# Two modulation blocks as dots instead of matmuls, five more groups of seven products, more adding transfers and a table of buffer places

## The chip, the cores and the metric

The kernel runs on one core of a Trainium2 chip, in one launch. The metric is the time on the device in microseconds, the median of several runs. A profile of one execution is there too, with the start and duration of every instruction; its span goes from the first to the last instruction.

## What is computed

One inference step of a transformer layer for two groups of 128 tokens, a prompt (context) and a sample (latent), both of width 2048 and with the same weights, all in float32:

```python
def ada_mod(cvec, w_ada, b_ada):
    m = jax.nn.silu(cvec) @ w_ada + b_ada
    return jnp.split(m, 6, axis=-1)
...
        sh1, sc1, g1, sh2, sc2, g2 = ada_mod(c_ctx[None, None, :], w_ada[l], b_ada[l])
        h = rms_norm(xp, norm1_w[l]) * (1 + sc1) + sh1
        qa, ka, va, qb, kb, vb, ga, gb = project_heads(h, w_in[l], q_norm_a[l], k_norm_a[l],
                                                        q_norm_b[l], k_norm_b[l])
...
        oa = context_attention(qa, ka, va, sink)
        ob = context_attention(qb[:, :, :, None, :], kb, vb, None)
        xp = xp + g1 * merge_branches(oa, ob, ga, gb, w_br_a[l], w_br_b[l], w_out[l])
        h2 = rms_norm(xp, norm2_w[l]) * (1 + sc2) + sh2
        xp = xp + g2 * sq_relu_mlp(h2, w_up[l], w_down[l])
```

The sample goes the same way, with a rotary on mixer A, a windowed and a neighbourhood mask, and cached context keys. The weights are `w_ada` (2048 x 12288), `w_in` (2048 x 8704), two branches (1024 x 2048 each), `w_out` (2048 x 2048), `w_up` (2048 x 8192) and `w_down` (8192 x 2048). Their elements pass through the core once, apart from the adding transfers below, which read a tile a second time.

## The kernel before

**Steps.** The work on the large weights is a list of steps (`wsteps`). A plain step takes one tile of 128 x 1024 floats (512 KB): two blocks of 128 rows by 512 columns. float32 is made of two parts: ScalarE copies the tile `raw` to a rounded `wH` (L115), VectorE takes the difference `wL` = `raw` - `wH` (L275), and the activations are split alike. Each product is then three matmuls, high x high, low x high and high x low (L477 to L479, L350 to L352, L1453 to L1455). For two blocks and two token groups a plain step has twelve matmuls of 128 x 512. Steps 0 to 72 are the first nine units of `w_in`, then come the gates (to 135), the branches `ya` and `yb` (136 to 167), `w_out` (168 to 199), and pieces of `w_up` and `w_down` in turn.

**Groups of seven.** From the second piece on, and in the last piece of `w_down`, two column blocks are made together (`pair`). Eight times two row blocks stand there; for each, the products of 2 x 2 blocks are either made plainly (eight products, two plain steps) or with seven products of sums of blocks (Strassen's and Winograd's scheme; the steps `x` and `y`), where `FAST` names the position. The sums cost VectorE and ScalarE work: `XL`, `t`, two sums in `raw`, the halves of `YB`, and the splits of `t` and `u` (L1521 to L1543).

**Adding transfers.** Instead of the subtraction on VectorE, ScalarE can write -`wH` into the tile and a DMA from GpSimd's (POOL's) queue adds the weight from memory (`minus_plus`):

```python
        act.activation(lo, hi.bitcast(F32), AF.Copy, scale=-1.0)
        pool.dma_start(lo, src.bitcast(F32R), accum_op=OP.add)
```

`LO_DMA` names plain steps and how many steps ahead this begins, `XL_DMA` and `T_DMA` the positions and leads for `XL` and for a sum, `YL_DMA` positions for half of `YB`. An entry whose step is no group of seven, or is prepared already, does nothing.

**Modulation.** Scale and shift of both norms and the gates come from `w_ada`. Two ways are used. With matmuls (`pair_mm`, L368): for one block of 128 features 16 matmuls of 256 columns, four of them side by side in quarters of the array, into `ps_ada`, later evacuated, transposed (`ps_sel`, L386) and added up (`ada_cols`). With dots (`dot`, L1746): VectorE multiplies a transposed tile of 128 x 1024 with the broadcast condition and adds up, once for each half of the 2048 inputs and each token group. `FB_DVE` is the block of the second modulation from which dots take over, 6 of 16. `SS_G` and `SS_AT` place the matmul blocks before it, `DOTS` the dots, both by steps. Most are in the time of the gates, the branches and `w_out`; `dot_end` closes the scale.

**Order.** The order on each engine is the order in which the code records: at each step `run` issues the loads up to `RUN` steps ahead on SP's queue, prepares tiles up to `LOOK` steps ahead (and `wH` alone for `AHEAD` more), then the matmuls, then what is placed at that step (`at`, `ex`): the work of the attention (`POST`, `JOBS`), dots and transposes. At the end of `w_out` norm2 takes its sum of squares (L1274), POOL the root `r` (L1276), VectorE and ScalarE `h2f` (L1284), PE transposes it (`ps_h`, L1292), and the scale of the second modulation is applied.

**Buffers.** 54 buffers of 128 x 1024 floats form one ring (`gp`, tag "g"); each new tile takes the place that is next in turn and waits until the tile before it there is done.

Of the kernel before, what the change touches and what calls it, by code (L numbers as in the profile page):

```python
# [34 lines left out]
FB_DVE = 6  # L35
# [12 lines left out]
YL_DMA = [8, 9, 15, 23, 29, 31, 39, 67]  # L48
T_DMA = {15: 10, 48: 10, 55: 7, 64: 7, 65: 7, 66: 7, 67: 11}
# [28 lines left out]
DOTS2 = [225, 231, 234, 235, 237, 238, 245, 245, 258, 266, 268, 270, 270, 294, 300, 301, 306, 327, 328, 331, 333, 336, 349, 359, 360, 362, 363, 367, 394, 395, 396, 401]  # L78
STAT_AT = [2, -1, 9, 1]
T_PAIR = [[14, 4], [6, 9], [8, 8], [5, 8], [8, 9], [5, 10], [6, 14]]  # L80
P_PAIR = [[5, -1], [1, 1], [0, 5], [1, 5], [1, 6], [0, 5], [2, 2]]
M_TE = (3,)
M_AT = [1, 2, 6]
FLIP = 1
SOW_AT = 3
# [1837 lines left out]
```

## Time and profile before

| | |
|---|---|
| Median of 3 runs | 1312.15 us (1312.04 to 1312.45) |
| Span of the profiled execution, first to last instruction | 1310.0 us; its own time with what lies around the span is not listed apart from the runs |
| Granted TensorE clock | 0.999 |
| Moved by DMA | 401.16 MB, mean 306 GB/s |
| DMA from SP's queue (q1) | 387.36 MB, 81.5% of the time of 16 DMA engines |
| DMA from POOL's queue (q0) | 12.59 MB, 34 transfers, 28 of them adding |

A busy share is the part of the span in which an engine had an instruction under way. Matmuls overlap, so their start times tell their price rather than their durations. In a row of a group, the numbers behind the count are the busy time in us and the mean ns of one; behind the second bar stands the idle time just before, and what ended it. In a row of waits: who waited for whom, us in total, how often, the longest.

### The profile page before, as it was taken

What the parts mean: (1) busy time and instruction counts of PE and PEld (TensorE: products, weight loads), DVE (VectorE), ACT (ScalarE), POOL (GpSimd) and SP (SyncE); (2) the same over time, 40 slices, a digit from 0 to 9 for tenths busy, and PEclk for the clock granted to TensorE, in tenths of its full rate; (3) what the DMA queues carried; (4) which work ended last, traced back from release to release, by engine and by line L of the source; (5) the groups of instructions that cost most, each with busy time, mean ns of one, the idle gap of its engine ahead of it and who ended that gap; (6) DMA issues with size and microseconds to landing.
All of it is one profiled execution on the core that took longest, in us unless ns stands there. A gap on an engine that the chain in (4) does not pass through costs nothing.

```text
span 1310.0 us, 17956 instructions
## 1 busy us (share of the span) xinstructions
PE 1301.6 (99%) x6328; PEld 1057.2 (81%) x6328; DVE 1141.7 (87%) x1466; ACT 908.8 (69%) x1151; POOL 59.2 (5%) x68
## 2 busy tenths in 40 slices
PE   8999999999999999999999999999999999999998
PEld 4778788788888878888888888888888888888887
DVE  4669799989999999999779998987999988789776
ACT  5635566699866655636787778869779597697882
POOL 0000000332000000000000000000000000000010
PEclk9999999999999999999999999999999999999999
DMA  9999999997799979997599788778977978879972
GB/s 371 408 409 408 400 409 399 354 318 227 265 345 367 370 284 366 358 334 244 193 307 318 210 286 268 283 261 273 321 229 245 357 255 281 295 225 349 337 246 72
DMA packets 169995, 401.16 MB, mean 306 GB/s; under 512 B 71697, under 2 KB 72689, under 8 KB 169905
## 3 DMA queue, kind: packets, MB, share of 16 engines
q1 hardware_dynamic: 165312, 387.36, 81.5%
q0 software_dynamic: 4448, 12.59, 5.4%
q8 instruction: 49, 0.80, 0.2%
q14 instruction: 42, 0.34, 0.1%
q10 hardware_dynamic: 144, 0.08, 0.1%
HBM read 374.23 MB, written 10.80 MB: 294 GB/s over the span
## 4 chain that ended last, share of the span: by engine, by line
PE 97%; DMA 1%; ACT 1%; SPq 0%; DVE 0%; issue 0%; ACTq 0%
PE acc L350 16%; PE acc L351 16%; PE acc L352 16%; PE Q L1453 7%; PE Q L1455 7%; PE Q L1454 7%; PE acc L477 5%; PE acc L478 5%; PE acc L479 5%; PE ps_ada L368 3%; DMA araw<-in_w_pair 1%; PE Z L1455 1%; PE Z L1453 1%; PE Z L1454 1%; PE ps_S L922 1%; PE acc L1233 1%
## 5 line engine op out<-in xcount | busy, mean ns | idle before, releaser
L275 DVE TENSOR_TENSOR wL<-raw,wH 128x1024 fp32r<-128x1024 f32 x375 | 440.7, 1221 | 44.5 <-ACT wH L115 43.0
L115 ACT ACTIVATE wH<-raw 128x1024 fp32r<-128x1024 f32 (+1 forms) x390 | 384.6, 1038 | 60.4 <-DMA raw<-in_w_in 15.0
L477 PE MATMUL acc<-wH,hH 128*128 128x512 f32 x272 | 107.2, 394 | 0.6 <-ACT srow L115 0.6
L478 PE MATMUL acc<-wL,hH 128*128 128x512 f32 x272 | 106.0, 390 | 0.0
L479 PE MATMUL acc<-wH,hL 128*128 128x512 f32 x272 | 106.0, 390 | 0.0
L350 PE MATMUL acc<-wH,hH 128*128 128x512 f32 x252 | 101.3, 402 | 0.0
L351 PE MATMUL acc<-wL,hH 128*128 128x512 f32 x252 | 98.4, 390 | 0.0
L352 PE MATMUL acc<-wH,hL 128*128 128x512 f32 x252 | 98.3, 390 | 0.0
L115 ACT ACTIVATE uH<-raw 128x1024 fp32r<-128x1024 f32 x36 | 38.2, 1062 | 53.8 <-DVE raw L1540 33.5
L1746 DVE CUSTOM_DVE_ANT_0 aT<-aT,cB,cols 128x1024 f32<-128x1024 f32 x56 | 71.5, 1285 | 0.6
L1746 DVE CUSTOM_DVE_ANT_0 junk<-aT,cB,cols 128x1024 bf16<-128x1024 f32 x56 | 71.3, 1281 | 0.0
L477 PEld LDWEIGHTS acc<-wH,hH 128*128 128x128 f32 x272 | 51.1, 188 | 14.1 <-issue 2.9
L479 PEld LDWEIGHTS acc<-wH,hL 128*128 128x128 f32 x272 | 51.1, 188 | 10.8
L478 PEld LDWEIGHTS acc<-wL,hH 128*128 128x128 f32 x272 | 51.1, 188 | 10.2
L350 PEld LDWEIGHTS acc<-wH,hH 128*128 128x128 f32 x252 | 47.4, 188 | 10.6 <-issue 1.4
L351 PEld LDWEIGHTS acc<-wL,hH 128*128 128x128 f32 x252 | 47.4, 188 | 10.5 <-DVE wL L275 0.6
L352 PEld LDWEIGHTS acc<-wH,hL 128*128 128x128 f32 x252 | 47.3, 188 | 10.0
L115 ACT ACTIVATE tH<-t 128x1024 fp32r<-128x1024 f32 x31 | 32.8, 1057 | 27.3 <-DVE t L1532 23.6
L1746 DVE CUSTOM_DVE_ANT_0 aT<-aT,cB,gc_g 128x1024 f32<-128x1024 f32 x32 | 40.8, 1284 | 0.4
L1746 DVE CUSTOM_DVE_ANT_0 junk<-aT,cB,gc_g 128x1024 bf16<-128x1024 f32 x32 | 40.7, 1282 | 0.0
L115 ACT ACTIVATE fTa<-pTa 128x2048 uint16<-128x2048 uint16 x16 | 40.6, 2536 | 0.1
L1433 ACT ACTIVATE up<-up 128x1024 f32<-128x1024 f32 x28 | 29.7, 1062 | 15.4 <-DVE up L1580 14.9
(739 smaller groups left out, 3377.6 us busy)
## 6 DMA issues: line engine op xcount, KB each, us to landing
raw<-in_w_in SPq DMA_DIRECT2D x131, 512.0 KB, 8.7
raw<-in_w_down SPq DMA_DIRECT2D x124, 512.0 KB, 7.2
araw<-in_w_pair SPq DMA_DIRECT2D x80, 512.0 KB, 9.8
raw<-in_w_upF SPq DMA_DIRECT2D x68, 512.0 KB, 6.2
aT<-in_w_gT SPq DMA_DIRECT2D x64, 512.0 KB, 7.8
raw<-in_w_up SPq DMA_DIRECT2D x60, 512.0 KB, 6.7
aT<-in_w_adaT SPq DMA_DIRECT2D x48, 512.0 KB, 8.0
raw<-in_w_out SPq DMA_DIRECT2D x32, 512.0 KB, 8.7
```

What stands on the lines that cost most here:

```text
L115: act.activation(out, in_, AF.Copy)
L275: dve.tensor_tensor(st["lo"], st["raw"], st["hi"].bitcast(F32), op=OP.subtract)
L350: pe.matmul(acc[tb], sh, wh[:, k, :], start=f, stop=False, **kw)
L351: pe.matmul(acc[tb], sh, wl[:, k, :], start=False, stop=False, **kw)
L352: pe.matmul(acc[tb], sl, wh[:, k, :], start=False, stop=l, **kw)
L477: pe.matmul(acc[tb], sh, wh[:, k, :], start=kt == 0 and k == 0 and not held and not seeded, stop=False, **kw)
L478: pe.matmul(acc[tb], sh, wl[:, k, :], start=False, stop=False, **kw)
L479: pe.matmul(acc[tb], sl, wh[:, k, :], start=False, stop=last and k == 1 and not hold, **kw)
L1453: pe.matmul(acc, stat[0], hi, start=f, stop=False, **kw)
L1454: pe.matmul(acc, stat[0], lo, start=False, stop=False, **kw)
L1455: pe.matmul(acc, stat[1], hi, start=False, stop=l, **kw)
L1746: dve.tensor_tensor_reduce(out, box["raw"], cB[s, tag], 1.0, dst if second else baT[:, part, fb:fb + 1], OP.mult, OP.add, dst)
```

## The change

- `FB_DVE` 6 to 4: blocks 4 and 5 of the second modulation, 32 matmuls of `ps_ada` and four transposes, become 16 dots. The last dot stands at step 190, before it was 183. The four other blocks, two at step 53 and two at step 73, are now at steps 52, 53, 69 and 73.
- `FAST`: 39 groups of seven among the 56 of pieces 1 to 7, before 34.
- The tables of adding transfers name 33 more places; the built program issues 24 more (10 `wL`, 4 `XL`, 8 halves of `YB`, 2 sums), 52 adding transfers in place of 28.
- `HOMES`: each tile of the ring gets a place of its own from a table, instead of the next in turn.
- Side work: in three units the squares for QK-norm are added up by ScalarE as it squares, head by head, instead of a reduction on VectorE (`SSQ_ACT`); two of the eight softmax normalisations go from VectorE to ScalarE (`NORM_ACT`); `LOOK`, `RUN`, `AHEAD`, `POST`, `JOBS`, `DOTS`, `DOTS2` and some smaller tables have new numbers.

```diff
-FB_DVE = 6
+FB_DVE = 4
...
-YL_DMA = [8, 9, 15, 23, 29, 31, 39, 67]
-T_DMA = {15: 10, 48: 10, 55: 7, 64: 7, 65: 7, 66: 7, 67: 11}
+YL_DMA = [8, 9, 11, 15, 16, 20, 23, 24, 27, 30, 37, 39, 44, 54, 55, 56, 61, 64]
+T_DMA = {11: 11, 15: 10, 21: 10, 31: 8, 38: 8, 43: 6, 48: 10, 64: 7, 65: 7, 66: 7}
...
-FAST = {1: (0, 1, 5, 7), 2: (0, 2, 3, 5, 7), 3: (0, 2, 3, 5, 7), 4: (0, 1, 3, 6, 7), 5: (0, 1, 3, 5, 7), 6: (0, 1, 3, 5, 7), 7: (0, 1, 3, 5, 7)}
+FAST = {1: (0, 1, 3, 5, 7), 2: (0, 1, 2, 5, 6, 7), 3: (0, 2, 3, 4, 6, 7), 4: (0, 1, 3, 4, 7), 5: (0, 3, 4, 6, 7), 6: (0, 1, 3, 5, 6, 7), 7: (0, 1, 4, 5, 6, 7)}
...
-LO_DMA = {186: 8, 205: 8, 218: 9, 357: 6, 402: 6, 415: 10, 451: 7, 455: 6}
+LO_DMA = {6: 7, 127: 6, 144: 6, 155: 6, 156: 12, 162: 10, 163: 6, 170: 6, 182: 8, 185: 6, 187: 7, 188: 7, 192: 10, 205: 8, 206: 9, 218: 7, 245: 10, 252: 9, 314: 9, 319: 7}
...
-SS_G = [(0, 2), (2, 1)]
-SS_AT = [53, 53, 73, 73, 125, 141]
+SS_G = [(0, 2)]
+SS_AT = [52, 53, 69, 73]
...
+HOMES = (
+    '0123456789:;<=>?@ABCDEFGHIJKLMNOPQRSTUVWXYZ[\\]^_`abcde789:;<=>4DEFG?@VTZAUB[YC]\\`_IH7eKLJMNOPQR98S<;:=@0?>S4ZDE<A:;@=S>?'
...
+SSQ_ACT = (('kB', 0), ('qA', 0), ('qA', 1))
+NORM_ACT = (('B', 0, 1), ('B', 1, 1))
...
+    homes = iter(HOMES)
+
+    def home():
+        return {"tag": f"g{ord(next(homes)) - 48}", "bufs": 1} if HOMES else {"tag": "g"}
+
     def G(name, dt=F32):
-        return gp.tile([P, 1024], dt, name=name, tag="g")
+        return gp.tile([P, 1024], dt, name=name, **home())
...
-        for s in range(2):
-            act.activation(sq[:, s].rearrange("p h d -> p (h d)"), raw[:, s, 0:nh * HD], AF.Square)
         ssq, r = SM(2 * nh, "ssq"), SM(2 * nh, "rq")
-        dve.tensor_reduce(ssq.rearrange("p (s h) -> p s h", s=2), sq, axis=AX.X, op=OP.add)
+        if u in SSQ_ACT:
+            for s in range(2):
+                for h in range(nh):
+                    act.activation(sq[:, s, h], raw[:, s, h * HD:h * HD + HD], AF.Square, accum_out=ssq[:, s * nh + h:s * nh + h + 1])
+        else:
...
-            dve.tensor_tensor(prob[:, :, 0:nk], prob[:, :, 0:nk], rd.unsqueeze(2).to_broadcast([P, 4, nk]), op=OP.mult)
+            if (mix, s, g) in NORM_ACT:
+                for h in range(4):
+                    act.activation(prob[:, h, 0:nk], prob[:, h, 0:nk], AF.Copy, scale=rd[:, h:h + 1])
+            else:
+                dve.tensor_tensor(prob[:, :, 0:nk], prob[:, :, 0:nk], rd.unsqueeze(2).to_broadcast([P, 4, nk]), op=OP.mult)
```

Three places show how this moves instructions. The first is on PE, in the second unit `yb` of the branches, where block 5 of the second modulation stood. Before (`oHB`, `oLB` are the parts of the attention's output, `ps_ada` the modulation's sums):

```order
L352 MATMUL acc<-wH,oLB_3837 128x512
L368 MATMUL ps_ada<-araw,cpad 32x256 x16
L350 MATMUL acc<-wH,oHB_4144 128x512
L351 MATMUL acc<-wL,oHB_4144 128x512
L352 MATMUL acc<-wH,oLB_4145 128x512
```

After, at the same place:

```order
L379 MATMUL acc<-wH,oLB_3900 128x512
L377 MATMUL acc<-wH,oHB_4161 128x512
L378 MATMUL acc<-wL,oHB_4161 128x512
L379 MATMUL acc<-wH,oLB_4162 128x512
L377 MATMUL acc<-wH,oHB_4161 128x512
```

The sixteen modulation matmuls are gone, and the branch's own matmuls follow each other directly.

The second is on POOL's queue, from the last store of a new key to the first pair; `r` is the root of norm2. Before:

```order
L846 DMA out_new_b_k<-u_kB_2299 128x512
L282 DMA wL<-in_w_out 128x1024
L282 DMA wL<-in_w_up 128x1024
L1276 TENSOR_TENSOR r<-ms,pw 128x1 x2
L282 DMA XL<-in_w_upF 128x1024
```

After:

```order
L878 DMA out_new_b_k<-u_kB_2346 128x512
L309 DMA wL<-in_w_in 128x1024
L309 DMA wL<-in_w_br_a 128x1024
L309 DMA wL<-in_w_br_b 128x1024
L309 DMA wL<-in_w_br_a 128x1024 x2
L309 DMA wL<-in_w_out 128x1024 x6
L309 DMA wL<-in_w_up 128x1024 x2
L1312 TENSOR_TENSOR r<-ms,pw 128x1 x2
L309 DMA XL<-in_w_upF 128x1024 x2
```

Thirteen adding transfers stand ahead of norm2's root, where there were two.

The third is on VectorE, from the last dot on the scale (`ISA` rows with `aT`; `scT` is the scale) to norm2's sum of squares `ss`. Before:

```order
L1746 ISA aT,scT_151<-aT,cB_3753,scT_151 128x1024
L1746 ISA scT_151 128x1
L275 TENSOR_TENSOR wL<-raw,wH 128x1024
L1752 SCALAR_TENSOR_TENSOR scT_151<-scT_151,cols 128x20
L275 TENSOR_TENSOR wL<-raw,wH 128x1024 x7
L1153 TENSOR_TENSOR t<-g_2_5489,acc 128x512
L1157 TENSOR_TENSOR x_2_4823<-x_2_4823,t 128x512
L275 TENSOR_TENSOR wL<-raw,wH 128x1024 x4
L1153 TENSOR_TENSOR t<-g_3_5622,acc 128x512
L1157 TENSOR_TENSOR x_3_5016<-x_3_5016,t 128x512
L1274 TENSOR_REDUCE ss<-ssq_435 128x1
```

After:

```order
L1782 ISA aT,scT_151<-aT,cB_3777,scT_151 128x1024
L1782 ISA scT_151 128x1
L302 TENSOR_TENSOR wL<-raw,wH 128x1024
L1788 SCALAR_TENSOR_TENSOR scT_151<-scT_151,cols 128x24
L302 TENSOR_TENSOR wL<-raw,wH 128x1024 x2
L1189 TENSOR_TENSOR t<-g_3_5652,acc 128x512
L1193 TENSOR_TENSOR x_3_5034<-x_3_5034,t 128x512
L1310 TENSOR_REDUCE ss<-ssq_435 128x1
```

Between the end of the dots and norm2 there are two subtractions now, and there were eleven.

More of the change, by code (lines that the diff above doesn't have):

```diff
@@ L66 @@
-CONST_AT = [73, 75]
-XL_DMA = {9: 8, 16: 10, 21: 7, 23: 9, 26: 7, 35: 9, 38: 11, 43: 9, 55: 10, 61: 8, 65: 2, 66: 11, 67: 10}
+LO_DMA = {6: 7, 127: 6, 144: 6, 155: 6, 156: 12, 162: 10, 163: 6, 170: 6, 182: 8, 185: 6, 187: 7, 188: 7, 192: 10, 205: 8, 206: 9, 218: 7, 245: 10, 252: 9, 314: 9, 319: 7}
+LOOK = "320000212520002000113432224544345446325343223485514450431655558056142666400217741254444407755554351165343464136341243646465067671214364840107565432464654678225497737202456687743027697899603788868561132011501887543981214635235427844640133987731746502100403354600601457981115649546317352668960005440033145620352043145664285243531423561358424543411423121401242333448325902337001253202436802600324526757331112130121225271003431223562215470383613565667359248785"
@@ L68 @@
+CONST_AT = [69, 74]
+XL_DMA = {8: 8, 9: 8, 16: 10, 18: 10, 21: 7, 23: 9, 27: 6, 29: 5, 30: 8, 31: 7, 35: 8, 37: 10, 38: 11, 43: 8, 48: 10, 51: 11, 53: 6, 55: 9, 59: 8, 65: 2, 66: 11}
 ADA_G = ((1,), (2,), (3, 4), (5, 6))
@@ L79 @@
+DOTS2 = [231, 231, 233, 234, 235, 237, 245, 246, 265, 268, 270, 270, 270, 298, 300, 300, 304, 330, 332, 333, 334, 347, 360, 360, 365, 366, 367, 367, 394, 395, 396, 401]
 STAT_AT = [2, -1, 9, 1]
-T_PAIR = [[14, 4], [6, 9], [8, 8], [5, 8], [8, 9], [5, 10], [6, 14]]
-P_PAIR = [[5, -1], [1, 1], [0, 5], [1, 5], [1, 6], [0, 5], [2, 2]]
+T_PAIR = [[14, 5], [6, 10], [8, 8], [5, 9], [9, 9], [5, 10], [5, 14]]
+P_PAIR = [[5, 2], [1, 2], [-1, 5], [1, 4], [0, 8], [1, 5], [2, 2]]
 M_TE = (3,)
@@ L814, in qk_stat @@
         sq = G("sq").rearrange("p (s h d) -> p s h d", s=2, d=HD)[:, :, 0:nh, :]
-        for s in range(2):
-            act.activation(sq[:, s].rearrange("p h d -> p (h d)"), raw[:, s, 0:nh * HD], AF.Square)
         ssq, r = SM(2 * nh, "ssq"), SM(2 * nh, "rq")
-        dve.tensor_reduce(ssq.rearrange("p (s h) -> p s h", s=2), sq, axis=AX.X, op=OP.add)
+        if u in SSQ_ACT:
[3 more added lines that the diff above has]
+        else:
+            for s in range(2):
+                act.activation(sq[:, s].rearrange("p h d -> p (h d)"), raw[:, s, 0:nh * HD], AF.Square)
+            dve.tensor_reduce(ssq.rearrange("p (s h) -> p s h", s=2), sq, axis=AX.X, op=OP.add)
         rsqrt(r, ssq, HD * EPS)
@@ L1049, in halves @@
     def halves(key, name):
-        return gp.tile([P, 2048], U16, name=f"{name}{key[0]}{key[1]}", tag="g")
+        return gp.tile([P, 2048], U16, name=f"{name}{key[0]}{key[1]}", **home())
     def part(key, src):
```

30 lines of the change are left out of this document (23 added, 7 removed).

## The prediction

> **What bounds the kernel now.** The page comes first: its span, and the engines' busy shares.
>
> ```profile
> span 1310.0 us, 17956 instructions
> PE 1301.6 (99%) x6328; PEld 1057.2 (81%) x6328; DVE 1141.7 (87%) x1466; ACT 908.8 (69%) x1151; POOL 59.2 (5%) x68
> ```
>
> TensorE is busy for all but 8.4 us. Its busy time could still hide waiting inside long matmuls, so the view of waits is next, for PE alone; it has five rows, of which these are the first and the last.
>
> ```profile
> PE ps_ss L174 <- ACT sq L171: 1.4, 1, 1.4
> ...
> PE ps_ada L368 <- DMA araw<-in_w_pair: 0.2, 1, 0.2
> ```
>
> All five are single waits, 3.9 us together, and all lie in the first 37 us: asked for from 40 us on, the view has no row. Third, the timeline of PE shows what a matmul costs when nothing waits.
>
> ```profile
> 421.15 0.39 PE L352 MATMUL acc<-wH,hL 128*128 128x512 f32 x1
> ...
> 421.83 0.39 PE L352 MATMUL acc<-wH,hL 128*128 128x512 f32 x1
> 422.15 1.93 PE L368 MATMUL ps_ada<-araw,cpad 128*32 128x256 f32 x32
> ...
> 424.58 0.39 PE L352 MATMUL acc<-wH,hL 128*128 128x512 f32 x1
> ```
>
> The start times count, not the durations, since matmuls overlap. From one L352 to the next (421.15 to 421.83) three matmuls take 0.68 us. So a step of twelve takes 4 x 0.68 = 2.72 us. The kernel is bound by the number of TensorE instructions: each one less is a gain, as long as the engines that prepare its operands keep up.
>
> How near those are to their limits, by stretch (PE, PEld, DVE, ACT, POOL busy, clock, share and GB/s of the DMA engines):
>
> ```profile
> 40.00:140.00 100.00, 100.00 (x675) 76.96 (x668) 72.74 (x105) 49.06 (x64) 0.00 (x0) 1.00 1.03 408
> 240.00:340.00 100.00, 100.00 (x533) 82.35 (x532) 92.01 (x135) 89.97 (x155) 26.97 (x25) 1.00 0.87 292
> 430.00:470.00 40.00, 40.00 (x201) 32.66 (x203) 38.48 (x53) 21.75 (x24) 0.00 (x0) 1.00 0.98 380
> 470.00:510.00 40.00, 40.00 (x188) 32.74 (x181) 37.24 (x50) 23.77 (x25) 0.00 (x0) 1.00 0.85 285
> 510.00:550.00 40.00, 40.00 (x182) 33.19 (x182) 39.48 (x55) 22.78 (x22) 0.00 (x0) 1.00 0.99 358
> 550.00:590.00 40.00, 40.00 (x178) 33.17 (x177) 38.90 (x51) 17.14 (x21) 0.95 (x1) 1.00 0.95 347
> 800.00:900.00 100.00, 100.00 (x443) 82.84 (x442) 86.27 (x99) 77.92 (x90) 2.63 (x3) 1.00 0.79 264
> ```
>
> PE is full in every stretch at clock 1.00. VectorE has 5.9 us idle in the 160 us from 430 on (160 less 154.1), 13.7 us in a later stretch of 100 us. The DMA engines are nearly always busy in both early stretches.
>
> **What PE loses.** *Groups.* A slow group is eight products of three matmuls, a group of seven has seven. Five groups change: 5 x 0.68 = 3.40 us less.
>
> *Modulation.* A visit of `ps_ada` for one block is 16 matmuls (32 records). In the rows above L352 to L352 across it is 424.58 - 421.83 = 2.75 us, less the 0.68 of the three ordinary matmuls: 2.07 us. A visit for two blocks, and the transposes that follow the last visit:
>
> ```profile
> 194.24 0.39 PE L479 MATMUL acc<-wH,hL 128*128 128x512 f32 x1
> 194.56 3.66 PE L368 MATMUL ps_ada<-araw,cpad 128*32 128x256 f32 x64
> ...
> 198.72 0.39 PE L479 MATMUL acc<-wH,hL 128*128 128x512 f32 x1
> 473.15 0.39 PE L352 MATMUL acc<-wH,oLB 128*128 128x512 f32 x1
> 473.38 0.60 PE L386 MATMUL ps_sel<-ident,S 128*128 128x128 f32 x4
> ...
> 474.29 0.40 PE L352 MATMUL acc<-wH,oLB 128*128 128x512 f32 x1
> ```
>
> Two blocks in one visit cost 4.48 - 0.68 = 3.80. Before, the second modulation has two visits of two blocks and two of one: 2 x 3.80 + 2 x 2.07 = 11.74 us. After it has four visits of one block (SS_AT 52, 53, 69, 73): 8.28. That is 3.46 us less; the split of the first two visits gives a part back. The removed four transposes are worth 1.14 - 0.68 = 0.46.
>
> Sum: 3.40 + 3.46 + 0.46 = 7.3 us. The profiled execution has a span of 1310.0; the median of the runs, 1312.15, has 2.15 us more around it, which no edit touches. So 1312.15 - 7.3 = 1304.8.
>
> **What the other engines get, and what hides it.**
>
> ```profile
> L1746 DVE CUSTOM_DVE_ANT_0 aT<-aT,cB,scT 128x1024 f32<-128x1024 f32 x12 | 15.4, 1284 | 0.0
> L818 DVE TENSOR_REDUCE ssq<-sq 128x8 f32<-128x1024 f32 x6 | 7.3, 1214 | 4.8 <-ACT sq L816 4.8
> L947 ACT ACTIVATE prob<-ps_S,nm 128x128 f32<-128x128 f32 x16 | 5.6, 364 | 2.6 <-DVE nm L945 2.0 <-DVE nm L943 0.6
> L947 ACT ACTIVATION_READ_ACCUMULATOR prob<-ps_S,nm 128x1 f32 x24 | 4.9, 202 | 0.0
> 602.24 8.04 DVE L275 TENSOR_TENSOR wL<-raw,wH 128x1024 fp32r<-128x1024 f32 x7
> 616.54 0.69 DVE L1153 TENSOR_TENSOR t<-g,acc 128x512 f32<-128x512 f32 x1 [0.39 <-PE acc L1250]
> 620.70 0.88 DVE L1284 TENSOR_SCALAR h2f<-x,r 128x512 f32<-128x512 f32 x2 [0.47 <-POOL r L1276]
> 624.51 1.03 PE L1292 MATMUL ps_h<-ident,h2f 128*128 128x128 f32 x8
> ```
>
> *VectorE to 616 us.* Added: two blocks, scale and shift, two halves, two streams, so 16 dots of 1.28 = 20.5 us. Gone: ten subtractions for `wL` at 8.04/7 = 1.15 (11.5), three reductions of 1.21 (3.6), and two softmax multiplies, worth between nothing and 2 x 1.21; I take half, 1.2, as one is half as wide. Net +4.2 us, in a time that PE shortens by the 3.9 us of the modulation: 8.1 us of idle time are needed. Idle are 8.0 us in 240:340 and 5.9 in 430:590. It fits, though not loosely, if the dots are spread over it, so I cost it at nothing. What is late if it doesn't fit is the residual at 616.54, behind which norm2, `h2f` and PE's transposes at 624.51 follow. There VectorE had 0.39 us to spare, and `h2f` was done at 621.58, 2.9 us before PE asked: 3.3 us of cover.
>
> *VectorE after 640 us.* A group of seven needs 1.15 each for `t`, `XL`, `tL`, `uL` and three halves of `raw` and `YB`, which I take at 0.6, half of it: 6.4 against 2.3 for a slow group's two `wL`. Five more: 20.5 us. The transfers take four `XL` (4.6), eight halves of `YB` (4.8) and about one half for each of two more `t` (1.1) away: net +10 us. At 13.7 idle us per 100, as in 800:900, some 630 us have 86: hidden, so it costs nothing; uncovered, it could take the groups' whole 3.4 us back.
>
> *ScalarE.* In three of the seven units the squares of 128x512 become 24 squares of 128x128 that add up by themselves; not in the trace in this form, bounded by the like exponentials: 24 x (0.364 + 0.202) = 13.6 us above, and nothing net below, since six squares go. Eight scaled copies replace VectorE's two multiplies, at 0.364 or a little more, some 3.5. In 240:340 ScalarE has 10 us idle; the three units are squared at steps 68 to 72, ahead of that stretch and in its first part. I take nothing, since the copies `wH` are made several steps ahead of PE (LOOK); without that cover 13.6 - 10 = 3.6 us would be short. The negative copies of ten `wL` fall where ScalarE is half idle.
>
> *Transfers.* The built program has 24 more adding transfers. Each waits for ScalarE's negative copy, and behind it on POOL's queue stand the next ones and, after those for `w_out` and `w_up`, norm2's `r`, for which VectorE waits at 620.70. The smallest lead that the tables give them is 6 steps, 16.3 us; copy, negative copy and issue take 3, and landing:
>
> ```profile
> raw<-in_w_upF SPq DMA_DIRECT2D x68, 512.0 KB, 6.2
> XL<-in_w_upF POOLq DMA_DIRECT2D x10, 512.0 KB, 7.3
> DMA packets 23611, 60.60 MB, mean 337 GB/s; under 512 B 8176, under 2 KB 8208, under 8 KB 23598
> q1 hardware_dynamic: 23454, 59.92, 90.7%
> q0 software_dynamic: 4448, 12.59, 5.4%
> SPq L246 <- PE acc L352: 34.0, 16, 8.8
> ```
>
> (The first two and the fifth row are the whole run's, the others 430:610.) 7.3 + 3 = 10.3 us, well inside 16.3. In bytes, 430:610 gets ten transfers of 0.524 MB: 60.60 + 5.24 = 65.84 MB in 180 us, 366 GB/s, under the 408 of 40:140, where PE waited for nothing. Hidden, at nothing. The dots load what the matmuls loaded.
>
> A page of the Trainium skill speaks against this: "DMA: Bandwidth & Descriptors", in the section on bandwidth, puts what one core gets from HBM at about 358 GB/s, and the fabric at 436. This trace has 408 over 100 us, so on this run the rule does not bind; the page ties its 358 to both cores of a memory domain streaming.
>
> *Places from a table.* PE waits for no buffer now, so nothing is to be gained there. SP does wait for buffers (34.0 us for PE's release in 430:610), which is why loads start when they do; a badly placed tile would hold the whole queue, by up to the 8.8 us that such a wait now lasts at most. I take nothing.
>
> **Rivals.** *VectorE late at 616 us.* If only the 1.6 us idle in 510:590 serve it, 8.1 - 1.6 - 3.3 = 3.2 us reach PE: 1308.0. For it: the last dots move back from step 183 to 190, and VectorE is 97 to 99% busy there. Against: the `wL` that stood behind them go to the transfers.
>
> *The adding transfers overfill the DMA engines, and it gets slower.* Place: 430:610. Over the run they take 5.4% of 1310 for 12.59 MB, 5.6 us per MB; ten take 29.4 us. The engines are free there for 7.4% of 180 (q1 90.7, q0 1.5, instruction queues 0.4), 13.3 us. Missing: 16.1 us, so 1320.9, and slower than before from 7.3 missing us on. Against: in 40:140 the share reads 1.03, so it counts queueing, and the bytes have room.
>
> *A rate limit.* If one core's loads were held to 358 GB/s there, 65.84 MB would take 183.9 us of a stretch that PE does in 176.1: 7.8 us, 1312.6, no change. The Trainium skill's page named above would give this.
>
> *The groups bring nothing.* If their operands come late in every new group, the 3.4 us are lost: 1308.2. Against: the idle time in 800:900.
>
> **How the numbers follow.** Forecast 1304.8: 0.68. VectorE late 1308.0: 0.12. Groups without gain 1308.2: 0.05. Rate limit 1312.6, or other losses that just cancel: 0.07. DMA engines overfilled 1320.9: 0.08. Faster by over 0.2% (2.6 us, about what a measurement of this kernel can tell) is under 1309.5: 0.85; within it 0.07; slower 0.08. The range goes from 1303.8, a microsecond below the sum for PE's changes of kind that I didn't count, to 1309.0, past the first two rivals.
>
> **What would show it.** Right: 32 fewer matmuls of `ps_ada` and 15 fewer of 128x512, PE's waits still none after 40 us. VectorE late: a wait of `ps_h` for `h2f`. Transfers: waits of PE for `wL`, `XL` or `YB` released by a DMA, landings well above 7.3 us. Wrong would be any wait of over 2 us on PE past 40 us, or a changed start.

## The result, and the profile after

The changed kernel takes **1333.7 us** (median of five runs, 1331.61 to 1336.68), the kernel before 1312.08 beside it: ratio 1.0167, 95% interval 1.0156 to 1.0178. It is 21.6 us slower, where 7.3 us less were forecast: 28.9 us are missing. The profiled execution took 1336.09, span 1334.3.

From the page of the changed kernel, the rows that answer to those of before:

```profile
span 1334.3 us, 18009 instructions
PE 1304.6 (98%) x6245; PEld 1055.9 (79%) x6245; DVE 1155.0 (87%) x1492; ACT 947.2 (71%) x1236; POOL 81.2 (6%) x92
q1 hardware_dynamic: 165312, 387.36, 80.7%
q0 software_dynamic: 7904, 22.55, 9.2%
```

PE has 83 records fewer, as it should (64 of `ps_ada`, 4 transposes, 15 matmuls of the groups), and yet is busy 3 us longer (at a lower clock, below) and idle for 29.7 us instead of 8.4. The view of PE's waits from 40 us on, which had no row before, now has nine (what waited, for whom: us in total, times, longest); these are the first five:

```profile
PE ps_T L1078 <- DVE g_gA L1144: 11.2, 2, 11.0
PE Q L1490 <- DMA YB<-in_w_upF: 3.3, 2, 2.8
PE Q L1489 <- ACT dsum L142: 2.1, 1, 2.1
PE Q L1489 <- ACT YB L142: 1.8, 1, 1.8
PE Q L1490 <- DVE tL L1578: 0.9, 1, 0.9
```

The prediction named "any wait of over 2 us on PE past 40 us" as the sign that it is wrong. There are three.

Where the time went, by the first matmul that reads a tile (us between starts in the trace, each row from the mark of the row above; the end is that of the last matmul). `m0H` and `m1H` are parts of the merged branches, which `w_out` reads, `ps_h` are norm2's transposes, and `a1H` to `a4H` are parts of what `w_down` reads; f1, g4 and f2 are experiments below:

| to the first matmul on | before | after | forecast | f1 | g4 | f2 |
|---|---|---|---|---|---|---|
| `m0H` (from the start) | 542.0 | 540.5 | 538.1 | 540.7 | 540.3 | 540.9 |
| `m1H` | 6.2 | 18.6 | 6.2 | 7.7 | 7.7 | 6.2 |
| `ps_h` (norm2) | 76.3 | 77.3 | 76.3 | 79.0 | 78.6 | 76.3 |
| `a1H` | 98.8 | 98.7 | 98.1 | 98.3 | 98.3 | 98.1 |
| `a2H` | 78.2 | 86.4 | 77.5 | 81.1 | 81.5 | 77.5 |
| `a4H` | 83.6 | 87.5 | 82.9 | 87.7 | 88.2 | 84.0 |
| end | 420.7 | 421.1 | 419.3 | 420.6 | 421.6 | 420.7 |

The marks sum to 31.7 us more than the forecast. Three places hold 25.9 of them: 12.4 ahead of `m1H`, 8.9 ahead of `a2H`, 4.6 ahead of `a4H`.

**The first place.** To transpose a tile of floats, the kernel splits it into planes of 16 bits (`plm`), SP's queue writes them transposed (`pTm`), and ScalarE joins them (`fTm`). The timelines of the changed kernel, at the third of these transposes by DMA for the merged branches; a row is start, duration, engine, line, operation, out<-in, count, and in brackets the idle time before it and what ended it. SP, before and then after:

```profile
525.20 2.62 SPq L1064 DMA_TRANSPOSE pTm<-plm  x1
```

```profile
530.87 8.62 SPq L1100 DMA_TRANSPOSE pTm<-plm  x1
```

POOL, 1.6 us later, the adding transfer of step 170:

```profile
532.48 0.88 POOL L309 DMA_DIRECT2D wL<-in_w_out  x1 [35.16 <-ACT wL L308]
```

ScalarE, VectorE and PE, which come behind one another:

```profile
550.77 2.48 ACT L142 ACTIVATE fTm<-pTm 128x2048 uint16<-128x2048 uint16 x1 [15.86 <-DMA pTm<-plm]
```

```profile
554.37 1.23 DVE L146 TENSOR_TENSOR m2L<-fTm,m2H 128x1024 fp32r<-128x1024 f32 x1 [14.56 <-ACT m2H L142]
```

```profile
557.07 1.09 PE L1078 MATMUL ps_T<-ident,g_gA 128*128 128x128 f32 x4 [10.98 <-DVE g_gA L1144]
...
559.70 0.63 PE L378 MATMUL acc<-wL,m1H 128*128 128x512 f32 x1
560.13 0.63 PE L379 MATMUL acc<-wH,m1L 128*128 128x512 f32 x1
...
562.33 0.39 PE L377 MATMUL acc<-wH,m1H 128*128 128x512 f32 x1
562.55 0.39 PE L378 MATMUL acc<-wL,m1H 128*128 128x512 f32 x1
```

The transpose lands 19.8 us after its issue; before, it took 4.4. ScalarE stands in its order at the copy `fTm`, VectorE at `m2L`, behind which the product of the gates (`g_gB`, `g_gA`) stands, and PE's transposes of that gate wait 11 us. Each engine works in its own order, so one late transfer stops all three. After the gap, matmuls start 0.43 us apart (559.70 to 560.13) rather than 0.22 (562.33 to 562.55): the granted clock is lower around the gap, 0.78 and 0.66 in the first two windows, and 1.00 in the third (the last columns are clock, DMA share, GB/s):

```profile
540.00:560.00 20.00, 8.78 (x37) 6.96 (x36) 5.56 (x8) 6.51 (x6) 0.00 (x0) 0.78 1.11 253
560.00:562.00 2.00, 2.00 (x7) 1.54 (x7) 2.00 (x4) 2.00 (x3) 0.00 (x0) 0.66 1.09 430
562.00:570.00 8.00, 8.00 (x37) 6.63 (x36) 8.00 (x11) 3.37 (x5) 0.00 (x0) 1.00 1.02 404
```

And what the DMA engines did in the middle of it (538 to 548 us: packets, bytes, mean rate, then packets, MB and share of the engines for SP's queue and for POOL's):

```profile
DMA packets 1554, 0.77 MB, mean 77 GB/s; under 512 B 1455, under 2 KB 1455, under 8 KB 1554
...
q1 hardware_dynamic: 1460, 0.41, 96.7%
q0 software_dynamic: 94, 0.36, 29.4%
```

Their time is taken (the shares add up to more than all of it, so they count waiting) and they move 77 GB/s. The loads that SP issued behind the transpose wait with it: the trace has ten of their packets in these 10 us.

### The profile page after: what moved, and what is told of

Read it like the earlier page. It is cut to its first block, busy times and chain, and to the rows that moved or that the text cites. A ratio compares the mean times of both kernels' runs of the same rounds, so it can differ in the third digit from the quotient of the medians.

```text
span 1334.3 us, 18009 instructions
## 1 busy us (share of the span) xinstructions
PE 1304.6 (98%) x6245; PEld 1055.9 (79%) x6245; DVE 1155.0 (87%) x1492; ACT 947.2 (71%) x1236; POOL 81.2 (6%) x92
## 4 chain that ended last, share of the span: by engine, by line
PE 77%; DMA 9%; DVE 6%; ACT 4%; issue 3%; POOL 0%; SPq 0%; DVEq 0%; ACTq 0%; POOLq 0%
PE acc L377 12%; PE acc L378 12%; PE acc L379 12%; PE Q L1490 5%; PE Q L1491 5%; PE Q L1489 5%; PE acc L504 5%; PE acc L506 5%; PE acc L505 5%; PE ps_ada L395 2%; DMA pTm<-plm 1%; DMA YB<-in_w_upF 1%; DVE junk L1782 1%; DMA araw<-in_w_pair 1%; ACT wH L142 1%
## 5 line engine op out<-in xcount | busy, mean ns | idle before, releaser
L302 DVE TENSOR_TENSOR wL<-raw,wH 128x1024 fp32r<-128x1024 f32 x355 | 416.8, 1220 | 29.5 <-ACT wH L142 29.1
L379 PE MATMUL acc<-wH,hL 128*128 128x512 f32 x252 | 98.3, 390 | 0.0
L1782 DVE CUSTOM_DVE_ANT_0 aT<-aT,cB,cols 128x1024 f32<-128x1024 f32 x60 | 76.3, 1290 | 0.4
L142 ACT ACTIVATE uH<-raw 128x1024 fp32r<-128x1024 f32 x41 | 43.5, 1062 | 46.4 <-DVE raw L1576 33.1
L1782 DVE CUSTOM_DVE_ANT_0 junk<-aT,cB,cols 128x1024 bf16<-128x1024 f32 x60 | 76.3, 1290 | 0.0
L506 PEld LDWEIGHTS acc<-wH,hL 128*128 128x128 f32 x272 | 51.1, 188 | 10.7
L505 PEld LDWEIGHTS acc<-wL,hH 128*128 128x128 f32 x272 | 51.1, 188 | 10.2
L142 ACT ACTIVATE tH<-t 128x1024 fp32r<-128x1024 f32 x34 | 35.9, 1055 | 24.1 <-DVE t L1568 20.1
L142 ACT ACTIVATE XH<-raw 128x1024 fp32r<-128x1024 f32 x41 | 42.7, 1048 | 2.1 <-PE Q L1490 1.6
L1578 DVE TENSOR_TENSOR tL<-t,tH 128x1024 fp32r<-128x1024 f32 x34 | 41.4, 1219 | 1.6 <-DMA pTa<-pla 1.6
L1579 DVE TENSOR_TENSOR uL<-raw,uH 128x1024 fp32r<-128x1024 f32 x34 | 41.7, 1225 | 1.1
L1568 DVE TENSOR_TENSOR t<-raw 128x1024 f32<-128x1024 f32 x34 | 41.4, 1219 | 1.0 <-DMA raw<-in_w_upF 0.7
## 6 DMA issues: line engine op xcount, KB each, us to landing
araw<-in_w_pair SPq DMA_DIRECT2D x72, 512.0 KB, 10.2
```

Source lines behind the costliest of these rows:

```text
L142: act.activation(out, in_, AF.Copy)
L302: dve.tensor_tensor(st["lo"], st["raw"], st["hi"].bitcast(F32), op=OP.subtract)
L379: pe.matmul(acc[tb], sl, wh[:, k, :], start=False, stop=l, **kw)
L505: pe.matmul(acc[tb], sh, wl[:, k, :], start=False, stop=False, **kw)
L506: pe.matmul(acc[tb], sl, wh[:, k, :], start=False, stop=last and k == 1 and not hold, **kw)
L1782: dve.tensor_tensor_reduce(out, box["raw"], cB[s, tag], 1.0, dst if second else baT[:, part, fb:fb + 1], OP.mult, OP.add, dst)
```

## Experiments

The experiments test four theories. A is a collision: a transfer of POOL's queue that meets a transpose by DMA (A1: only one that adds, A2: any). B is the table of places, C the bytes to move, D VectorE. e2, f1, f2, g1, g2 and h4 leave one term of some low parts out and show times alone; the others compute everything.

e1 was to make the tile of step 170, whose transfer meets the transpose, by a subtraction on VectorE in the same place; this order of work deadlocks, and there is no time for it. g4 below comes to the same thing.

**e2, e3, e4: adding or not, another place, the kernel before.** e2 (changed kernel):

```diff
+        if st["i"] in LO_COPY:          # (170,)
+            act.activation(st["lo"], st["hi"].bitcast(F32), AF.Copy, scale=-1.0)
+            pool.dma_start(st["lo"], st["src"].bitcast(F32R))
+            return
         minus_plus(st["lo"], st["hi"], st["src"])
```

> The changed kernel, with the transfer of step 170 issued on the same queue, with the same bytes and the same waits, but written over the tile rather than added to it (one weight tile's low part is then wrong by the high part). If it is the adding that collides with the transpose (theory A1): transpose 4.4 to 10 us, time 1320 to 1325. If any transfer of POOL's queue does it (A2): transpose over 14 us, time 1330 to 1337.

Transpose 16.3 us, 1331.23 (1327.66 to 1335.67). So a plain transfer does it too: A2.

e3 (changed kernel): `YL_DMA` without 16, and

```diff
-                    minus_plus(b["XL"], b["XH"], b["x"]["src"])
+                    if 8 * p + pos in XL_DVE:          # (16, 18)
+                        dve.tensor_tensor(b["XL"], b["x"]["raw"], b["XH"].bitcast(F32), op=OP.subtract)
+                    else:
+                        minus_plus(b["XL"], b["XH"], b["x"]["src"])
```

> The changed kernel, with three adding transfers near the transpose of 753 us (XL of the groups 16 and 18, YB of group 16) made by subtractions on VectorE again. Theory A: that transpose lands in 4.3 to 6 us, not 11.8; the loss between the first matmuls on a1H and a2H (86.4 us apart, 78.2 before) falls from 8.2 us to under 2, and the time by 6 to 9 us, to 1325 to 1328. Theory C: VectorE has 3.1 us more to do there and the same loads come as late: the loss stays over 6 us, the time within 3 us of 1333.7.

From `a1H` to `a2H` 81.9 us rather than 86.4, half of the loss. But 1338.72 (1334.86 to 1340.6): the transpose of 531 us, which the edit doesn't touch, took 24.8 us in this profile. The length of the collision is not fixed, and its spread hides what e3 was to show.

e4 (kernel before):

```diff
-LO_DMA = {186: 8, ...
+LO_DMA = {170: 6, 186: 8, ...
```

> The kernel before, with one adding transfer more: step 170, of the same tile of w_out as in the changed kernel, six steps ahead. Theory A: where it comes to lie beside the third transpose of the merged gate (525 us), the transpose takes over 9 us, PE waits 4 to 12 us ahead of the gate's own transposes (547 us), and the time rises by 4 to 13 us, to 1316 to 1325. Theories B and C (and A, if the transfer starts after the transpose has landed): within 1.5 us of 1312.1.

1313.06 (1312.49 to 1313.7), ratio 1.0005 (0.9996 to 1.0015). POOL issued it at 533.6 us, after the transpose had landed (525.4 + 4.6), so it says nothing on A, and against C only that one transfer more is free.

**f1 to f4: take it away, take 45 away, provoke it, the places.** f1 (changed kernel) leaves the transfer of step 170 out:

```diff
+        if st["i"] in LO_NONE:          # (170,)
+            act.activation(st["lo"], st["hi"].bitcast(F32), AF.Copy, scale=-1.0)
+            return
         minus_plus(st["lo"], st["hi"], st["src"])
```

> The changed kernel, with the transfer of step 170 left out (the low part of that tile of w_out is then minus its high part); all else as it was. Theory A, as the runs so far leave it (any transfer of POOL's queue in flight beside a transpose by DMA on SP's queue, adding or not, holds both up, by a time that differs from run to run: 16.3, 19.8 and 24.8 us in three profiles): the third transpose of the merged gate lands in 8 to 11 us (its issue alone took 8.6 us), PE's gap ahead of the gate's transposes falls from 11.4 to between 0.3 and 3 us with no slow clock behind it, and the time to 1319 to 1324. Theories B (places) and C (bytes to move): gap over 8 us, time 1330 to 1335.

1322.75 (1321.06 to 1327.76), **11 us less for one of the 45 transfers that `minus_plus` issues** (the other seven of the 52 add a block to a sum). The tile's view for that transpose in f1 (least, median and most of one):

```profile
DMA to landing us min/median/max: 8.9/8.9/8.9
```

The stretch to `m1H` goes from 18.6 to 7.7 us, and no slow matmuls follow. A holds; B and C can't explain this.

f2 (changed kernel):

```diff
         act.activation(lo, hi.bitcast(F32), AF.Copy, scale=-1.0)
-        pool.dma_start(lo, src.bitcast(F32R), accum_op=OP.add)
```

> The changed kernel, with the adding transfer left out in all places where it makes a low part (weights, XL, YB; those that make a sum stay); ScalarE's copies with minus stay, so the low parts there are minus the high parts. Theory A: all transposes land in 3 to 10 us, the gaps at 557, 777 to 797 and 900 us are gone, and the groups, the two blocks and the transposes left out show what the prediction said: 1303 to 1309. Theory B: the places still make SP late: over 1320. Theory C: the bytes of the adding transfers (0.5 MB for each of 28 tiles, 0.25 MB for each of 17 halves) are gone as well, so 1303 to 1309 too, but with the gap at 557 us closed only if f1 closes it as well.

1310.36 (1309.63 to 1311.4), ratio 0.9986 (0.9976 to 0.9995). This leaves out all 45 transfers of `minus_plus`, of which the kernel before has 23 as well; the seven that add to a sum stay. The three large losses are gone but for 1.1 us ahead of `a4H`; what PE still waits for from 40 us on is small (three of five rows):

```profile
PE Q L1489 <- DVE uL L1578: 0.8, 1, 0.8
PE acc L376 <- ACT acc L142: 0.7, 1, 0.7
PE acc L377 <- DVE wL L302: 0.7, 2, 0.5
```

So 23.3 of the 28.9 us come with these transfers; the other 5.6 are there without them.

f3 (kernel before): `LO_DMA` with `170: 10`.

> The kernel before, with the one adding transfer of step 170, ten steps ahead rather than six, so that POOL issues it at about 523 us, ahead of the third transpose (525.2 us), and not after its landing. Theory A: the transpose lands 9 to 25 us after its issue, not 4.4, PE waits 3 to 15 us ahead of the gate's transposes, 1315 to 1329. If the collision needs SP's queue to be full of loads as well (the third transpose's issue took 2.6 us before, 8.6 us after the change): transpose under 8 us, time within 2 us of 1312.1.

1312.89, ratio 1.0002 (0.9993 to 1.0012). POOL issued at 520.9 us, the transfer was in flight when the transpose (525.4) was issued, and the transpose landed in 6.8 us rather than 4.4. A transfer that is ahead of the transpose does little harm: POOL's packets ran until 529 us, the transpose's after them. The expectation's other reading, that SP's queue must be full of loads as well, came out with its numbers (under 8 us, no change of time) and isn't refuted by this run; the table below bears on it.

f4 (changed kernel): `HOMES = ()`.

> The changed kernel with the table of places emptied, so that its 54 buffers are given out in turn as before the change. Theory B (the table makes SP's loads late): faster, under 1325, with shorter waits of SP and the transposes under 10 us. Theory A: the adding transfers stay, so the losses stay or move with the new times; 1328 to 1345. If the table helps, it is slower than 1333.7 by what it helps.

1343.15 (1338.34 to 1347.87), with the same collision (19.4 us). The table of places doesn't cause the loss; it saves 9.5 us.

**g1 to g4.** In the changed kernel the transpose of 753 us landed after 11.8 us, and VectorE and ScalarE came late behind it. g1 is f1, and ScalarE's copy with minus alone also for `XL` of groups 16 and 18 and `YB` of 16.

> Run f1_without_170 again, with the transfers of XL of groups 16 and 18 and of YB of group 16 left out as well (those low parts are minus the high parts). In f1 the stretch from the first matmul on a1H to the first on a2H took 81.1 us, in f2_no_adds 77.5, in the kernel before 78.2. If these three transfers (757 to 762 us in the changed kernel, behind a transpose) are what makes it long: under 78.7 us, no wait of PE over 1 us between 760 and 805 us, and 2 to 3.5 us less than f1, 1318.5 to 1321. If it is the weight's transfer at 742 us or those of 780 to 793 us, or VectorE: over 80 us and the time of f1.

77.7 us from `a1H` to `a2H` (f1 81.1): these three are the cause of what f1 still loses there. The time is 1321.78 all the same (1318.9 to 1322.82), as in this profile another pair met worse: a transpose issued at 686.8, a transfer 1.6 us later, landing 13.5 us (8.2 in f1), and ahead of `a1H` 103.2 us, where f1 has 98.3.

g2 is f1, and the same for `XL` of group 31.

> Run f1_without_170 again, with the transfer of XL of group 31 left out as well, the first of three that POOL issues within 1.6 us (887 us in the changed kernel) and whose last, YB of group 30, PE waits for. From a3H to a4H: 82.2 us in f1, 78.5 in f2_no_adds, 78.2 before. If the three stand in line (each 0.5 MB by adding takes the 16 engines about 2.6 us: 128 packets of 328 ns): YB lands in about 8 us, not 10.9, PE waits under 1 us for it, the stretch takes under 79.5 us and the time 2.5 to 4 us less than f1, 1318.5 to 1320.5. If YB is late because its issue is late (the engines ahead of it): it still waits over 2 us, and the time is f1's.

Stretch 81.2 us, the wait for `YB` at 886 us 1.8 rather than 2.8, time 1322.74 (1321.71 to 1323.03): a miss, the line of three is the lesser part. For the rest see h2.

g3 (kernel before):

```diff
-FB_DVE = 6
+FB_DVE = 4
-SS_G = [(0, 2), (2, 1)]
+SS_G = [(0, 2)]
...
```

> The kernel before with the modulation part of the change alone (FB_DVE, SS_G, SS_AT, DOTS, DOTS2 and CONST_AT as in the changed kernel): two blocks by dots on VectorE. The prediction's step: two visits of 64 matmuls less and nothing late: 3.0 to 3.9 us less than before, 1308.5 to 1309.5. Rival (VectorE late ahead of the gate at 616 us and of the modulation's own use): 1310.5 to 1313.

**1328.03** (1327.17 to 1329.13), ratio 1.0119 (1.0103 to 1.0136): 15.6 us slower, not 3 faster. PE's waits from 40 us on:

```profile
PE ps_gr L1759 <- DVE gc_g L1746: 5.5, 1, 5.5
PE acc L1193 <- DVE wL L275: 3.1, 2, 1.9
PE acc L351 <- DVE wL L275: 2.7, 2, 1.6
PE acc L1249 <- DVE wL L275: 2.5, 2, 1.8
```

All are for VectorE, and its windows (third time) are full:

```profile
430.00:485.00 55.00, 53.86 (x238) 44.28 (x236) 54.79 (x75) 28.82 (x31) 0.00 (x0) 1.00 0.88 333
...
560.00:627.00 67.00, 61.40 (x267) 49.42 (x266) 66.28 (x89) 28.57 (x36) 0.95 (x1) 1.00 0.87 310
```

g4 (changed kernel): `LO_DMA` with `170: 4`, four places adapted.

> The changed kernel with the adding transfer of step 170 four steps ahead rather than six (LO_DMA 170: 4; four tiles that are given out in another order for it get other places), so that it starts 5 us later and meets the transpose when most of it has landed. Nothing is left out. Theory A: the transpose lands in 8 to 12 us, PE's gap ahead of the gate's transposes is under 3 us, 1320 to 1326. If the collision is not a matter of when POOL issues it: over 14 us, 1329 to 1337. If the transfer now comes too late for its own use: a wait of PE for wL of 2 us or more at about 550 us.

1324.84 (1322.21 to 1325.89), the transpose 9.0 us, 7.7 us to `m1H`: 8.9 us are back. But the transfer doesn't start later, as the edit was meant to do; it is gone. Four steps ahead, this tile already stands in VectorE's order, so the entry does nothing: POOL's queue has 57 transfers instead of 58, none between 510 and 560 us, and VectorE one subtraction for `wL` more (366 for 365). So g4 is f1 with everything computed, and says nothing on the moment. It is the best complete version with the change, and slower than before (ratio 1.0092, 1.0077 to 1.0107).

**h1 to h4: the parts alone.** h1 (kernel before): `FAST` of the changed kernel.

> The kernel before with the change's groups alone (FAST as in the changed kernel, with before's transfers, as far as they fall on groups of seven, and its buffers in turn). The prediction's step (0.68 us for each of five groups, VectorE's added work hidden in 86 us of idle time): 3 to 3.4 us less, 1309.0 to 1309.5. Rival (VectorE or the operands late in the new groups, as its order of work is another): 1311 to 1320.

**1332.68** (1330.49 to 1334.17), ratio 1.0154 (1.0139 to 1.0169), 20.2 us slower. (Two entries of before's tables fall on no group of seven here, so 26 transfers add, not 28.) The largest wait is 5.2 us for ScalarE's `dsum` at 769 us, and ScalarE in turn waited for VectorE. The same 50 us in h1 and in the kernel before (PE, PEld, DVE, ACT, POOL):

```profile
720.00:770.00 50.00, 44.77 (x197) 36.84 (x196) 48.97 (x62) 38.67 (x42) 0.87 (x1) 0.99 0.73 233
```

```profile
720.00:770.00 50.00, 50.00 (x223) 41.40 (x222) 47.42 (x58) 41.62 (x44) 1.75 (x2) 1.00 0.75 239
```

Before, VectorE had 2.6 us to spare here; by the prediction's estimate one group asks for 4.1 more. Room is not the whole of it: from 1100 to 1200 us PE loses 4.7 us in h1 while VectorE is busy for 83.0 of 100, and VectorE waits for ScalarE (`wH` 5.8 us) as ScalarE does for it (`raw` 13.9). There the order of work, still that of before, looks like the limit; no run tests it.

h2 is g4 with `YL_DMA` without 30.

> Run g4_170_lead4 again (1324.8, the stretch from a3H to a4H 82.7 us), with YB of group 30 made by VectorE, not by an adding transfer; nothing is left out. If PE's wait there is for a transfer that is issued too late (7.8 us ahead of its use in the changed kernel, where it took 10.9): the wait is gone, the stretch takes 78 to 79 us, and the time is 3 to 4.5 us less, 1320 to 1322. If what is ahead of it (VectorE, ScalarE) is late itself: PE waits for VectorE's YB or uL there, over 2 us, and the time is g4's.

From `a3H` to `a4H` 79.2 us (g4 82.7), with no wait for this `YB`: the transfer had been issued too late. The median, 1324.94 (1319.51 to 1325.69), is g4's: the profiled run has a transpose of 16.0 us at 743 us, beside three transfers, and from `a1H` to `a2H` 86.8 us, where g4 has 81.5.

h3 (changed kernel): `HOMES = ()`, and `LO_DMA`, `YL_DMA`, `XL_DMA`, `T_DMA` as before.

> The changed kernel with its buffers in turn (as f4_ring, 1343.2) and with the tables of transfers of the kernel before (LO_DMA, YL_DMA, XL_DMA, T_DMA), so that VectorE does the work of the 24 new transfers. If the transfers are what costs, even with the work back on VectorE: under 1325. If VectorE needs that relief more than the transfers cost (as g3 suggests, 16 us for the modulation alone): over 1325, PE waiting for VectorE's wL and gc_g.

1335.9 (1334.35 to 1340.89): over 1325, the rival's side, with PE waiting for VectorE (`gc_g` 2.8 us, `wL` 2.8) and for ScalarE's `dsum` (9.9); but 7.2 us under f4. With buffers in turn, the new transfers cost more than the work they take away. The old ones are not free of the collision: in this profile, the slowest of the four runs, a transpose issued at 754 us took 19.7 us, with a transfer 0.9 us behind it.

h4 is g4 without the transfers of steps 182, 185, 187, 188 and 192.

> Run g4_170_lead4 again, with the transfers of the five weight tiles of w_out at 574 to 602 us (steps 182, 185, 187, 188, 192) left out (low parts minus the high parts). If these transfers make the loads and so VectorE late: PE's waits at 547, 610 and 627 us (0.6, 0.3 and 1.5 us) go to under 0.5 us in all, and the time falls by 2 to 3 us, to 1322 to 1323. If VectorE is late for the dots: they stay, and the time is g4's, 1324 to 1326.

1325.03 (1324.88 to 1325.82). The waits ahead of 612 us shrink, and `m0H` to `ps_h` goes from 86.3 to 85.3 us; the wait of `ps_h` for VectorE's `h2f` stays at 1.4. The time is g4's, as expected for a VectorE that is late with the dots. The five cost about 1 us there.

**k1, k2: POOL waits for each transpose.** k1 (changed kernel):

```diff
         sync.dma_start_transpose(planes[key][:, 0:n].rearrange("p (j t) -> p j t", t=P), pl[:, 0:n])
         beside[0] = BESIDE
+        pool.tensor_copy(SM(1, "seen"), planes[key][:, 0:1])
```

> The changed kernel with one small copy on POOL behind each transpose by DMA, of one column of the transposed tile, so that POOL issues no transfer while a transpose that was issued ahead of it is in flight; nothing is left out. Theory A (a transfer that POOL issues after a transpose's issue and before its landing holds both up): no transpose after 430 us takes over 10.7 us (the most of 223 transposes without such a transfer in the profiles so far; 77 with one went up to 24.8), PE's gap at 557 us is under 2 us, the runs lie within 2.5 us of one another (5.1 us for the changed kernel), and the time is 1317 to 1324. Rival (it is the bytes and their queue, not the meeting): the transfers now come later still, PE waits for YB and XL by DMA over 6 us in all, 1326 to 1336.

The transfer of step 170 is issued at 540.8 us, behind the transpose's landing (9.3 us after 530.7), and the stretch to `m1H` takes 7.5 us with nothing left out. So at the first of the three places the moment decides. No transpose after 430 us takes over 10.2 us (three still have a transfer issued 0.5 to 3.3 us behind them), and still the time is 1332.67 (1329.85 to 1334.25): A's signs and the rival's time. PE's waits for transfers (two rows):

```profile
PE Q L1491 <- DMA YB<-in_w_upF: 9.7, 2, 5.7
PE acc L378 <- DMA wL<-in_w_out: 1.5, 1, 1.5
```

A transfer that is held until the transpose has landed comes later, and `YB` had no time to give. Behind the gaps from 540 to 910 us some 40 matmuls start 0.33 to 0.6 us apart rather than 0.23, which adds about 8 us (an estimate from the start times; the granted clock of 540 to 560 us is 0.83).

k2 is k1 with `YL_DMA` without 16, 27, 30, 55 and 61.

> Run k1_pool_waits again, with five of the YB halves (groups 16, 27, 30, 55, 61), which PE uses 6.5 to 11.4 us after the issue of their transfers, made by VectorE; nothing is left out. If these are late by their issue: 2 to 4.5 us less than k1, PE's waits for YB by DMA under 1 us in all. If VectorE is late with them instead: waits of PE for YB, uL or ScalarE's dsum take their place, and the time is k1's within 1.5 us.

1332.86 (1331.78 to 1333.96), no gain: 4.0 us of waiting for a `YB` that is still transferred stay, and 3.7 us for ScalarE's `acc` are new.

**All transposes after 430 us together**, in the 17 profiles before, after and e2 to h4, by what POOL's queue did:

| POOL's transfer | transposes | landing, us: least, median, most |
|---|---|---|
| none in flight | 223 | 4.2, 4.5, 10.7 |
| issued ahead of the transpose | 23 | 4.3, 6.0, 9.9 |
| issued after it, ahead of its landing | 77 | 4.3, 8.3, 24.8 |

All fifteen over 11.5 us are of the last kind, the first such transfer 0.9 to 4.3 us behind the transpose. The step up to 10.7 without any comes with a long issue on SP: of the 223, those whose issue alone took over 4 us (48) took 6.0 to 10.7.

So a transfer behind the transpose isn't enough. Of the 77, the 34 whose issue took up to 4 us landed within 9.0; all fifteen slow ones have an issue of 4.4 us or more, their own packets began 2.4 to 5.1 us after its start (in the changed kernel at 531 us after 4.0, and SP's earlier loads move until then), and packets of POOL's queue came in between. The kernel before has three transposes with an issue of 1.3 to 2.0 us and a transfer 1.6 to 2.9 us behind it: they landed in 4.3 to 4.6 us, with no packet of POOL's between theirs. That both are needed, a transpose that waits behind SP's loads and a transfer of POOL's that comes up meanwhile, is what the profiles have in common; no run changes SP's queue alone.

## Why the prediction was wrong, step by step

**What bounds the kernel** was right as far as it went: PE, and every instruction less is time, as long as the operands come. **Groups**, 0.68 us each: in f2 the stretches ahead of `a1H` and `a2H` are 0.7 us shorter each. Right there; in the two stretches with the other three groups f2 gains nothing (0.3 us longer and the same, where 0.7 and 1.4 less were forecast), with waits of 0.7 us for `acc` in the one and 0.8 for `uL` in the other. **Modulation and transposes**, 3.46 and 0.46: between the same matmuls on `acc`, the stretch with the first of the two visits that went (the 1500th to the 1600th) is 2.1 us shorter. The one with the second visit and the four transposes (the 1700th to the 1800th) is 1.8 us shorter, with a new wait of 0.6 for the gate's `gc_g` in it, and the two split visits give back 0.4 each. That is 3.2, and 3.8 without the wait, of 3.9: right. What wasn't counted is the attention's time: from the 900th to the 1300th of these matmuls PE has as many instructions as before and takes 1.3 us longer, 0.7 of it waits for `wL`, in another order of work. Which edit of the side work makes this was not tried. With 0.4 us at the start, where the loads of the first blocks differ from run to run, and the wait for `gc_g` this makes up the first row of the table, 2.4 us.

**The step that failed is that on transfers**: "The smallest lead that the tables give them is 6 steps, 16.3 us ... well inside 16.3 ... Hidden, at nothing." Three things in it were wrong.

First, it took the landing of a transfer for its whole effect. Nothing in the sum asked what a transfer does to the others. f1 and g4 show 11 and 8.9 us for one transfer that isn't issued, and k1 the same place without the loss when it is issued later. The trace of before had the warning: its eleven transposes by DMA up to 405 us had taken 3.0 to 10.9 us, so their landing wasn't fixed. The prediction asked what holds SP's queue, but not for the transposes in it.

Second, `YB` has no lead. `YL_DMA` is a list, not a table with steps: the transfer is issued where the tile is made. In the changed kernel the trace has 6.3 to 11.4 us from a `YB` transfer's issue to PE's first use of the tile, and 3.9 to 10.9 to its landing. For `YB` of group 30 PE was ready for it after 7.8, and it landed after 10.9, the last of three transfers that POOL issued in a row:

```profile
886.95 0.86 POOL L309 DMA_DIRECT2D XL<-in_w_upF  x1 [6.70 <-DMA raw<-in_w_down]
887.87 0.88 POOL L1539 DMA_DIRECT2D raw<-in_w_upF  x1
888.55 1.09 POOL L309 DMA_DIRECT2D YB<-in_w_upF  x1
```

h2 takes it away and has 3.5 us back. For `wL` the least from issue to use was 10.5 us, where 16.3 less 3 for what comes ahead of the issue should have left 13.3.

Third, the bytes. In 430:610, the stretch of the rival that would have it slower, the changed kernel's queues read

```profile
q1 hardware_dynamic: 22147, 55.64, 88.0%
q0 software_dynamic: 1430, 5.24, 15.6%
```

103.6% together, against 92.2 before. That is the rival's place and sign, but not its mechanism: from `m0H` to `ps_h` the changed kernel loses 13.5 us against f2, and f1, with nine of the ten transfers (102.8%), 4. That 13.5 is near the rival's 16.1 is luck.

**VectorE to 616 us** ("It fits, though not loosely"): with nothing else in its way it fits to the last us. In f2:

```profile
430.00:560.00 130.00, 129.43 (x581) 107.08 (x580) 129.51 (x171) 82.52 (x82) 0.00 (x0) 1.00 0.97 353
560.00:600.00 40.00, 40.00 (x178) 33.14 (x177) 40.00 (x60) 21.08 (x28) 0.00 (x0) 1.00 0.91 337
```

That left no cover: in f1 and g4 VectorE loses a few us to a late transpose (4.3 us at `m2L` in f1), and ends 1.4 us late for `ps_h`, the rival named at 616 us, on top of the rest. **VectorE after 640 us** ("some 630 us have 86: hidden") was wrong in kind. Idle time of a long stretch can't be spent in one place: h1, the groups without new transfers, is 20.2 us slower, and g3, the modulation alone, 15.6. So each part needs what else the change does to VectorE's work, and the price of that was put at nothing as well. These are not pure prices of the two parts: both runs keep the side work and the order tables that were made for the old work, and no run has the transfers' work back on VectorE with a table of places made for it.

**Places**, at nothing: they save 9.5 us (f4), in the changed kernel.

The sum as measured, us: 7.3 forecast; against it 12.4 for the collision at 531 us; 8.9 ahead of `a2H`; 4.6 ahead of `a4H`; 1.0, 0.6 and 1.8 in the other stretches; 2.4 up to `m0H`. That is 24.3 more than before in the profiled run, which lies 2.4 above the median. Of the 8.9, f1 has 3.6 left, and g1 shows that these come with the three transfers behind the transpose; why the other 5.3 go when only the transfer of step 170 is left out, 200 us ahead, no run shows. Of the 4.6, h2 shows 3.5 for the late `YB`, and 1.1 are in f2 too.

## What to carry to other kernels

A transfer that is hidden for its own use can still be in the way of another: list what is in flight beside it, transposes by DMA above all, and ask who stands in order behind those. Idle time counts where and when the work falls, not over a stage; if two edits lean on the same cover, do one alone first. Look in the trace whether an edit did what it was meant to: in g4 the transfer that was to be moved had vanished. And where a table gives leads, read in the trace from issue to use; a list without leads has the lead that the code's order leaves.

## What the runs showed of the hardware

**A transpose by DMA and a transfer of another queue.** Alone, the transpose's packets of 256 bytes take 18 ns (the third one of before: some 2000 in 3 us). In the collision of the changed kernel they come in bursts: from 538 to 548 us the median is 18 ns still, but from 538 to 539 us only 27 come, of 0.67 us (median), twice the 0.327 us of POOL's packets of 4 KB there; in e2, where these take 0.173, up to 0.35 from 538 to 540 us. That suggests that the packets of the two queues wait for one another; why it lasts so long while so little moves is not shown by any run. The Trainium skill, "DMA: Bandwidth & Descriptors", section "Rules for kernel authors", says that a transpose next to ordinary DMAs needs nothing, in a rule against corrupted results. For the results no run here speaks against it; for the time the table above differs, 24.8 us at most against a median of 4.5, and the measurement decides.

**An added byte costs the engines two.** A packet of 4 KB takes 159 to 164 ns as a load and 327 to 328 when it is added; in e2, written plainly from the same queue, 173. So the 0.52 MB of a tile by adding hold the 16 engines for 128 x 328 / 16 = 2.6 us, where a load takes 1.3.

**A gap on PE costs more than itself.** After the gap of 11.4 us five matmuls start 0.43 us apart, about 1 us lost; after the gaps of 776 to 791 us (2.5, 2.2, 0.7 and 1.3 us) there are twelve such, 2.4 us. The Trainium skill, "TensorE: Matmul & The Clock Gate", section "Wait — 56ns, not 53.3ns?", has 426.7 ns for 512 columns at the low clock; the trace agrees (426 to 428).
